# Sums of the gates' right operands formed behind two value blocks instead of in four attention units

## The chip, the core and the metric

One core of a Trainium2 chip runs the whole block. The time is the device time of one execution, in microseconds, and the figure that counts is the median of several. The engines are TensorE (PE, with its weight loads as PEld), VectorE (DVE), ScalarE (ACT), GpSimd (POOL) and SyncE (SP, which here only issues transfers). Each engine works through its own instructions in order; an instruction that waits holds all that stand behind it on its engine.

## The reference

One decoder block on x of 1024 rows (S) by 1024 channels (D), float32, with two attention branches of 512 channels each:

```
h    = rms_norm(x, g_pre)
proj = h @ w_in                          # q, k, v, z of both branches, forget logits, gates
ya   = fox_attention(qa, ka, va, log_sigmoid(fa + b_forget)) * silu(za)      # 8 heads of 64
yb   = diff_attention(rope(qb), rope(kb), vb, lam)                           # 4 heads, 2 x 64
yb   = rms_norm(yb, g_subln) * (1 - lam_init) * silu(zb)
gate_a, gate_b = split(sigmoid(gates))                                       # 1024 columns each
y    = (gate_a * (ya @ w_branch[0]) + gate_b * (yb @ w_branch[1])) @ w_out
out  = x + rms_norm(y, g_post)
```

All products are wanted to float32 accuracy. The kernel splits each operand into a high part (a cast) and a low part (the operand minus the cast), and adds three matmuls: high by high, high by low, low by high.

## The kernel before

**Value stage** (to about 112 us). `x_block(i)` normalizes 128 rows, transposes them and splits them into `hT`: eight tiles of 128 partitions by 4 by 512, indexed by part (high, low), half of the channels (kh) and half of the rows of x (sh). `v_block(i)` (L183 on) multiplies 128 rows with the value and forget columns, 72 matmuls into three accumulators `pv`, and brings the result out: ACT casts the high parts (L201, L207), DVE subtracts the low parts (L202, L208), SP stores `vbs` and `vas`. A loop over i calls `x_block(i + 3)` and `v_block(i)`, so all of `hT` is there once `v_block(4)` is reached. Blocks are counted from 0 in the code. The weights of this stage came through four slots of the pool `xp` named `wvraw`, which nothing uses after the weights are split.

**Attention** (to about 593 us). Eight units, 0 to 3 diff and 4 to 7 fox. `unit_proj(u)` multiplies the columns of q and k in two halves each (accumulators `pk`, `pq`, L246; two buffers `pj`; weights split by `load_w`, L234 and L236). For diff units `rope` copies the accumulator out and adds a rotated copy that SP moves between partitions; `stack` (L295 to L298) makes TA, TB, KA and KB. Each query row then has its score matmuls (`Sd` or `Sf`, L426) with a fused reduction on DVE (L428), an exponential on ACT (L433), scaling on POOL (L519, L549), transposes on PE (L455), and a product with the values (L479). The projections of the next unit, the products for z and, in fox units, other small tasks stand in a list `fill` that is worked off between the rows, to give PE something to do. Which instruction comes where on each engine is decided by a scheduler before the launch, from the order of the code, priorities and a simulated timeline; so a moved task moves its neighbours too.

**The combinations.** `h_combinations(k)` (L360 to L385), one for each k of 0 to 3, forms four sums or differences of the four quarters of h for one row tile of 128 channels: T5 = f12 - f11, T7 = f22 - f12, T6 = f22 - T5's tile, T4 = f21 - T6's tile, in the code's names, where each f is the sum of a high and a low quarter, made on POOL (L364). ACT casts the high part (L370), DVE makes the low part (L371), and SP stores each part by itself, 256 KB, in `t_d` in HBM (L373). The tiles are `raw` (three slots) and `sw` (two slots) of the pool `stg`, which the attention's own work shares. `TFILL` puts one call into the third place of `fill` in each of units 4 to 7.

**Gates.** `h_load` (L810) reads T4 to T7 back, 1 MB for each part, and the gate projections from the second on use them as right operands of a seven-product scheme in place of eight.

Of the kernel before, what the change touches and what calls it, by code (L numbers as in the profile page):

```python
# [9 lines left out]
F32 = mybir.dt.float32  # L10
F32R = mybir.dt.float32r
AF = mybir.ActivationFunctionType
ALU = mybir.AluOpType
# [3 lines left out]
P = 128  # L17
# [4 lines left out]
CH = 512  # L22
NEG = -1.0e30
SKEW = 1
SFILL = ((), (), (), (0,), (1,), (2,), (3,), ())
TFILL = ((), (), (), (), (0,), (1,), (2,), (3,))
UPR, DNR = slice(0, 64), slice(64, 128)
UP, DN = (0, 1, 2, 3), (3, 2, 1, 0)
GORD = (UP,) * 4 + (DN,) * 4
# [12 lines left out]
def f32(ap):  # L42
    return ap.bitcast(F32)
# [3 lines left out]
def tile_hybrid_block(  # L47
# [18 lines left out]
    nc = tc.nc  # L66
# [8 lines left out]
    dram = ctx.enter_context(tc.tile_pool(name="dram", bufs=1, space=DRAM))  # L75
# [21 lines left out]
    hT = [[[hpool.tile([P, 4, CH], F32R, tag=f"h{part}{kh}{sh}", name=f"hT{part}{kh}{sh}")  # L97
            for sh in range(2)] for kh in range(2)] for part in range(2)]
# [6 lines left out]
    ss_d = dram.tile([4, S], F32, name="ss_d")  # L105
    rs_d = dram.tile([4, S], F32, name="rs_d")
    z_d = [dram.tile([P, S], F32, name=f"z_d{t}") for t in range(8)]
    t_d = {m: [dram.tile([P, 4, CH], F32, name=f"t_d{m}_{part}") for part in range(2)]
           for m in (4, 5, 6, 7)}

    def rstd_of(dst, ss, n, eps):
        nc.gpsimd.tensor_scalar(dst, ss, 1.0 / n, eps, op0=ALU.mult, op1=ALU.add)
# [6 lines left out]
    with ExitStack() as st:  # L119
        vw = st.enter_context(tc.tile_pool(name="vw", bufs=1))  # L120
        xp = st.enter_context(tc.tile_pool(name="xp", bufs=2))
# [32 lines left out]
        def x_block(i):  # L154
            xs = wpool.tile([P, D], F32, tag="wraw", name=f"xs{i}")
            xg = xp.tile([P, D], F32, tag="xg", name=f"xg{i}", bufs=2)
            ss = small.tile([P, 1], F32, tag="ss", name=f"ss{i}")
            rs = small.tile([P, 1], F32, tag="rs", name=f"rs{i}")
            if i == 0:
                for half, acc in enumerate((rs, ss)):  # L160
                    hs = slice(half * CH, (half + 1) * CH)
                    nc.sync.dma_start(xs[:, hs], x2[0:P, hs])
                    nc.scalar.activation(xg[:, hs], xs[:, hs], AF.Square, accum_out=acc)
                nc.gpsimd.tensor_tensor(ss, ss, rs, op=ALU.add)
            else:
                nc.sync.dma_start(xs, x2[i * P:(i + 1) * P, :])
                nc.scalar.activation(xg, xs, AF.Square, accum_out=ss)
            rstd_of(rs, ss, D, EPS)
            for half in range(2):
                hs = slice(half * CH, (half + 1) * CH)  # L170
                nc.vector.scalar_tensor_tensor(
                    xg[:, hs], xs[:, hs], rs, g_bc[:, hs], op0=ALU.mult, op1=ALU.mult)
                tp = tps.tile([P, CH], F32, tag="tp", name=f"xt{i}_{half}")
                for q in range(4):
                    k = half * 4 + q
                    nc.tensor.transpose(tp[:, q * P:(q + 1) * P], xg[:, k * P:(k + 1) * P], ident)
                sl = slice(i % 4 * P, (i % 4 + 1) * P)
                tv = tp.rearrange("p (k s) -> p k s", k=4)
                hh, hl = (hT[part][half][i // 4][:, :, sl] for part in range(2))
                nc.scalar.copy(hh, tv)  # L180
                nc.vector.tensor_tensor(hl, tv, hh, op=ALU.subtract)  # L181

        def v_block(i):  # L183
# [26 lines left out]
            nc.vector.tensor_tensor(fg[:, i, :], ps[2][:, 256:264], bf_bc, op=ALU.add)  # L210
            nc.sync.dma_start(va_d[sl].rearrange("s a (b c) -> s (a b) c", b=2), f32(sa))

        x_block(0)
        for k in range(KT):
            load_wv(k)
# [3 lines left out]
        for i in range(NB):  # L219
            if i + 3 < NB:  # L220
                x_block(i + 3)
            v_block(i)


    def load_w(name, src, hi_act=False, lo_pool=False, pieces=None):
# [25 lines left out]
    with ExitStack() as st:  # L251
# [93 lines left out]
        def sum_squares(t, c):  # L345
# [10 lines left out]
            nc.tensor.matmul(ps, lhsT=onesr, rhs=lo, start=False, stop=True)  # L356
            nc.scalar.copy(sq[0:1], ps[0:1])
            nc.sync.dma_start(ss_d[t:t + 1, sl], sq[0:1])

        def h_combinations(k):  # L360

            def full(nm, kh, sh):
                t = stg.tile([P, CH], F32, tag="raw", name=f"f{nm}_{k}", bufs=3)
                nc.gpsimd.tensor_tensor(t, hT[0][kh][sh][:, k, :], hT[1][kh][sh][:, k, :], op=ALU.add)  # L364
                return t

            def parts(m, t):
                hi, lo = (stg.tile([P, CH], F32R, tag="sw", name=f"t{m}_{k}_{part}")
                          for part in range(2))
                nc.scalar.copy(hi, t)  # L370
                nc.vector.tensor_tensor(lo, t, hi, op=ALU.subtract)  # L371
                for part, p in enumerate((hi, lo)):
                    nc.sync.dma_start(t_d[m][part][:, k], f32(p))  # L373

            f11, f12 = full("11", 0, 0), full("12", 0, 1)
            nc.vector.tensor_tensor(f11, f12, f11, op=ALU.subtract)
            parts(5, f11)
            f22 = full("22", 1, 1)
            nc.vector.tensor_tensor(f12, f22, f12, op=ALU.subtract)
            parts(7, f12)  # L380
            nc.vector.tensor_tensor(f11, f22, f11, op=ALU.subtract)
            parts(6, f11)
            f21 = full("21", 1, 0)
            nc.vector.tensor_tensor(f21, f21, f11, op=ALU.subtract)
            parts(4, f21)  # L385

        def subln_scales(t):
            rs = sub_rs[:, t]
# [237 lines left out]
        for u in range(8):  # L626
            load, load_v, groups = nxt or unit_attn(u, T)
            nxt = None
            if u == 0:
                vload.append(load_v)  # L630
            if u == 1:
                forget_sums()
            load()
            fill = []
            if u + 1 < 8:
                T, tasks = unit_proj(u + 1)
                fill += tasks
            for t in ZFILL[u]:
                fill += z_tasks(t)
            fill[2:2] = [lambda k=k: h_combinations(k) for k in TFILL[u]]  # L640
            for t in SFILL[u]:
                fill += [lambda t=t, c=c: sum_squares(t, c) for c in range(2)]
                fill.append(lambda t=t: subln_scales(t))
            total = sum(s[0] for s in groups)
            done, nf = 0, 0
            for n, (wgt, rws, prd) in enumerate(groups):
                if n == len(groups) // 2 and u < 7:
                    nxt = unit_attn(u + 1, T)
                    vload.append(nxt[1])
                for r in rws:  # L650
                    r()
                if pend:
                    pend()
                pend = prd
                done += wgt
                while nf < len(fill) and nf < len(fill) * done / total:
                    fill[nf]()
                    nf += 1
# [145 lines left out]
    def h_load():  # L804

        ts = {m: [tpool.tile([P, 4, CH], F32R, tag=f"T{m}{part}", name=f"T{m}{part}")
                  for part in range(2)] for m in (6, 4, 7, 5)}
        for m in (4, 6, 5, 7):
            for part in range(2):
                nc.sync.dma_start(f32(ts[m][part]), t_d[m][part])  # L810
            h_ops[m] = [[t[:, k, :] for k in range(4)] for t in ts[m]]

    def gates_pair(d, order):
# [227 lines left out]
```

## Time and profile before

| | us |
|---|---|
| runs | 938.9, 936.02, 934.56 |
| median | 936.02 |
| span of the profiled execution | 932.1 |
| median less span | 3.9 |
| PE busy in the span | 890.1 |
| DVE, ACT, POOL busy | 625.5, 436.0, 486.6 |
| value stage ends (last `pv` matmul) | 111.7 |
| attention ends, gates begin | 593 |

The time of an execution holds the span, which is what the trace shows, and some microseconds around it that the trace does not show. In the rows of a timeline stand the start, the length, the engine, the line, the operation with what it writes and reads, and in brackets how long the engine had been idle before it and what ended that. A row of the waits names an engine and a line, what it waited for, and the total, the times and the longest. A row of groups has the busy total and the mean length in ns. A row of a table by stage has the stretch, its length, busy time and number of instructions on PE, PEld, DVE, ACT and POOL, the granted clock, the share of the DMA engines and GB/s.

### The profile page before, as it was taken

What the parts mean: (1) busy time and instruction counts of PE and PEld (TensorE: products, weight loads), DVE (VectorE), ACT (ScalarE), POOL (GpSimd) and SP (SyncE); (2) the same over time, 40 slices, a digit from 0 to 9 for tenths busy, and PEclk for the clock granted to TensorE, in tenths of its full rate; (3) what the DMA queues carried; (4) which work ended last, traced back from release to release, by engine and by line L of the source; (5) the groups of instructions that cost most, each with busy time, mean ns of one, the idle gap of its engine ahead of it and who ended that gap; (6) DMA issues with size and microseconds to landing.
All of it is one profiled execution on the core that took longest, in us unless ns stands there. A gap on an engine that the chain in (4) does not pass through costs nothing. (4 is left out here: it accounts for less than half of the span.)

```text
span 932.1 us, 13768 instructions
## 1 busy us (share of the span) xinstructions
PE 890.1 (95%) x4600; PEld 748.2 (80%) x4600; DVE 625.5 (67%) x1185; ACT 436.0 (47%) x861; POOL 486.6 (52%) x456
## 2 busy tenths in 40 slices
PE   7999999989999999999999998999999999999994
PEld 5899987777887878888878887788888878887873
DVE  6731257788878778577667568425668792559776
ACT  3421125556667574564755657523434450323331
POOL 7200034634745467373644566417677436878961
PEclk9999999999999999999999999999999999999997
DMA  8542346425334253544444342596655595211242
GB/s 314 185 139 93 114 124 160 115 69 138 98 92 142 71 179 104 157 128 124 147 153 129 98 161 72 221 396 193 197 167 174 184 362 198 71 44 46 91 135 90
DMA packets 118664, 136.95 MB, mean 147 GB/s; under 512 B 10545, under 2 KB 84273, under 8 KB 117570
## 3 DMA queue, kind: packets, MB, share of 16 engines
q1 hardware_dynamic: 118450, 135.82, 46.0%
q8 instruction: 36, 0.59, 0.3%
q14 instruction: 34, 0.28, 0.1%
q10 hardware_dynamic: 144, 0.26, 0.1%
HBM read 85.65 MB, written 37.81 MB: 132 GB/s over the span
## 5 line engine op out<-in xcount | busy, mean ns | idle before, releaser
L195 PE MATMUL pv<-wvhi,hT 128*128 128x264 f32 (+2 forms) x384 | 89.7, 326 | 0.4 <-DVE hT L181 0.4
L246 PE MATMUL pz<-hT,hi_z 128*128 128x512 f32 x256 | 83.9, 394 | 0.0
L246 PE MATMUL pk<-hT,hi_k 128*128 128x512 f32 x256 | 81.2, 394 | 2.0 <-DVE KB L298 2.0
L246 PE MATMUL pq<-hT,hi_q 128*128 128x512 f32 x256 | 82.3, 394 | 0.2 <-DVE TB L298 0.2
L727 PE MATMUL x_o<-wo_op,a_o 128*128 128x512 f32 x336 | 78.0, 392 | 3.4 <-POOL a_o L679 2.2
L861 PE MATMUL pb<-yT,hi_br 128*128 128x512 f32 x256 | 78.8, 390 | 0.1
L727 PEld LDWEIGHTS x_o<-wo_op,a_o 128*128 128x128 f32 x336 | 62.8, 188 | 18.5 <-POOL a_o L679 3.1
L727 PE MATMUL x_g<-T,a_g 128*128 128x512 f32 x336 | 77.5, 390 | 0.0
L727 PEld LDWEIGHTS x_g<-T,a_g 128*128 128x128 f32 x336 | 63.1, 188 | 13.3
L195 PEld LDWEIGHTS pv<-wvhi,hT 128*128 128x128 f32 x384 | 64.9, 191 | 6.3 <-DVE hT L181 0.7
L549 POOL TENSOR_SCALAR Pf<-Pf,lf 128x1024 f32<-128x1024 f32 (+3 forms) x64 | 50.2, 787 | 29.5 <-DVE lf L435 24.6
L433 ACT ACTIVATE Pd<-Pd,mxd 128x128 f32<-128x128 f32 (+7 forms) x64 | 49.6, 775 | 33.9 <-DVE mxd L428 33.2
L519 POOL TENSOR_SCALAR Pd<-Pd,ld 128x128 f32<-128x128 f32 (+7 forms) x32 | 26.1, 816 | 73.6 <-DVE ld L518 41.4
L545 POOL TENSOR_TENSOR cb<-cb,trim 128x128 f32<-128x128 f32 x64 | 31.1, 488 | 61.0 <-DVE mxf L428 39.8
L433 ACT ACTIVATE Pf<-Pf,mxf 128x1024 f32<-128x1024 f32 (+3 forms) x64 | 49.7, 777 | 27.3 <-DVE mxf L428 24.6
L195 PE MATMUL pv<-wvlo,hT 128*128 128x512 f32 (+2 forms) x192 | 62.0, 325 | 0.0
L727 PE MATMUL x_g<-hT,a_g 128*128 128x512 f32 x252 | 58.6, 390 | 0.0
L246 PEld LDWEIGHTS pk<-hT,hi_k 128*128 128x128 f32 x256 | 47.3, 188 | 12.0 <-DVE KB L298 2.4
L459 DVE TENSOR_TENSOR plf<-ptf,phf 128x512 fp32r<-128x512 f32 (+1 forms) x80 | 49.8, 633 | 10.2 <-ACT phf L458 9.7
L861 PEld LDWEIGHTS pb<-yT,hi_br 128*128 128x128 f32 x256 | 48.0, 188 | 10.5 <-DVE cu_g L720 0.6
L727 PEld LDWEIGHTS x_g<-hT,a_g 128*128 128x128 f32 x252 | 47.3, 188 | 10.0
L246 PEld LDWEIGHTS pq<-hT,hi_q 128*128 128x128 f32 x256 | 47.4, 188 | 9.4 <-PE pk L246 0.5
(247 smaller groups left out, 2419.4 us busy)
## 6 DMA issues: line engine op xcount, KB each, us to landing
t_d<-t SPq DMA_DIRECT2D x32, 256.0 KB, 2.1
T<-t_d SPq DMA_DIRECT2D x8, 1024.0 KB
raw<-in_w_in_dram SPq DMA_DIRECT2D x14, 512.0 KB, 4.2
vb_d<-vbs SPq DMA_DIRECT2D x8, 512.0 KB
va_d<-vas SPq DMA_DIRECT2D x8, 512.0 KB, 4.0
raw_k<-in_w_in_dram SPq DMA_DIRECT2D x8, 512.0 KB, 4.2
raw_q<-in_w_in_dram SPq DMA_DIRECT2D x8, 512.0 KB
V<-vb_d SPq DMA_DIRECT2D x4, 1024.0 KB
```

The source lines that it names most:

```text
L195: nc.tensor.matmul(ps[n], lhsT=hT[hp][k // 4][i // 4][:, k % 4, hs], rhs=wt[k][:, a:b], start=first, stop=(k == KT - 1 and hp == 1))
L246: nc.tensor.matmul(ps, lhsT=a[:, k, :], rhs=hT[h][k // 4][c][:, k % 4, :], start=(k == 0 and a is hi and h == 0), stop=(k == KT - 1 and a ...
L433: nc.scalar.activation(pr[:, 0:n], pr[:, 0:n], AF.Exp, bias=mx[:, len(pcs) - 1:len(pcs)], scale=-1.0, accum_out=le)
L459: nc.vector.tensor_tensor(pl[:, 0:n], pt[:, 0:n], ph[:, 0:n], op=ALU.subtract)
L519: nc.gpsimd.tensor_scalar(p2[:, 0:n], p2[:, 0:n], l2, 1.0, op0=ALU.mult, op1=ALU.mult)
L545: nc.gpsimd.tensor_tensor(diag, diag, trim, op=ALU.add)
L549: nc.gpsimd.tensor_scalar(p1[:, 0:n], p1[:, 0:n], l1, 1.0, op0=ALU.mult, op1=ALU.mult)
L727: nc.tensor.matmul(x[m], lhsT=a[:, ai, k, :], rhs=right[m][bi][k], start=(k == 0 and n == 0), stop=(k == 3 and n == 2))
L861: nc.tensor.matmul(ps, lhsT=a[:, kk, :], rhs=yT[g][h][:, k % 2, sl], start=(k == 0 and a is hi and h == 0), stop=(k == 3 and a is lo))
```

## The change

`h_combinations` moves into the value stage. `TBLK` calls it for k = 0 and 1 behind `v_block(4)` and for k = 2 and 3 behind `v_block(5)` (value blocks 5 and 6, counted from 1). The arithmetic is the same: per row tile 4 adds on POOL, 4 subtractions and 4 low parts on DVE, 4 casts on ACT. The tiles come from the four `wvraw` slots: `fa` and `fb` hold two f each, and each T has one tile with both parts. One transfer of 512 KB stores an operand's tile, 16 in place of 32, and it is issued from ACT's queue and not from SP's. In HBM both parts of an operand stand in one array, and `h_load` reads the same bytes.

```diff
-TFILL = ((), (), (), (), (0,), (1,), (2,), (3,))
+TBLK = ((), (), (), (), (0, 1), (2, 3), (), ())
...
-    t_d = {m: [dram.tile([P, 4, CH], F32, name=f"t_d{m}_{part}") for part in range(2)]
-           for m in (4, 5, 6, 7)}
+    t_d = {m: dram.tile([P, 2, 4, CH], F32, name=f"t_d{m}") for m in (4, 5, 6, 7)}
...
+        def h_combinations(k):
+
+            fa = xp.tile([P, 2, CH], F32, tag="wvraw", name=f"fa_{k}", bufs=4)
+            fb = xp.tile([P, 2, CH], F32, tag="wvraw", name=f"fb_{k}", bufs=4)
+            f11, f12, f22, f21 = fa[:, 0], fa[:, 1], fb[:, 0], fb[:, 1]
+
+            def full(t, kh, sh):
+                nc.gpsimd.tensor_tensor(t, hT[0][kh][sh][:, k, :], hT[1][kh][sh][:, k, :], op=ALU.add)
+
+            def parts(m, t):
+                p = xp.tile([P, 2, CH], F32R, tag="wvraw", name=f"t{m}_{k}", bufs=4)
+                nc.scalar.copy(p[:, 0], t)
+                nc.vector.tensor_tensor(p[:, 1], t, p[:, 0], op=ALU.subtract)
+                nc.scalar.dma_start(t_d[m][:, :, k], f32(p))
+
+            full(f11, 0, 0)
+            full(f12, 0, 1)
+            nc.vector.tensor_tensor(f11, f12, f11, op=ALU.subtract)
+            parts(5, f11)
...
             v_block(i)
+            for k in TBLK[i]:
+                h_combinations(k)
...
-        def h_combinations(k):
...
-                hi, lo = (stg.tile([P, CH], F32R, tag="sw", name=f"t{m}_{k}_{part}")
-                          for part in range(2))
-                nc.scalar.copy(hi, t)
-                nc.vector.tensor_tensor(lo, t, hi, op=ALU.subtract)
-                for part, p in enumerate((hi, lo)):
-                    nc.sync.dma_start(t_d[m][part][:, k], f32(p))
...
-            fill[2:2] = [lambda k=k: h_combinations(k) for k in TFILL[u]]
...
-                nc.sync.dma_start(f32(ts[m][part]), t_d[m][part])
+                nc.sync.dma_start(f32(ts[m][part]), t_d[m][:, part])
```

The lines behind the diff's first part have other numbers in the changed kernel (L201 becomes L200, L236 becomes L265, L298 becomes L327). The scheduler's order moves at three places that the prediction speaks of. First ACT's order from the fifth value block on (`vbs4`, `vas4`: the evacuations of block 4). Before:

```order
L201 CAST vbs4_854<-pv4_0_779 128x4x128
L207 CAST vas4_858<-pv4_1_780 128x4x64
L207 CAST vas4_858<-pv4_2_781 128x4x64
L201 CAST vbs5_940<-pv5_0_865 128x4x128
L207 CAST vas5_944<-pv5_1_866 128x4x64
```

and the same place in the changed kernel, where a DMA row is the issue of a store:

```order
L223 CAST t5_0_866<-fa_0_861 128x512
L225 DMA t_d5_134<-t5_0_866 256x1x512
L223 CAST t7_0_872<-fa_0_861 128x512
L200 CAST vbs4_850<-pv4_0_775 128x4x128
L225 DMA t_d7_136<-t7_0_872 256x1x512
L223 CAST t6_0_877<-fa_0_861 128x512
L206 CAST vas4_854<-pv4_1_776 128x4x64
L225 DMA t_d6_135<-t6_0_877 256x1x512
L223 CAST t4_0_883<-fb_0_862 128x512
L206 CAST vas4_854<-pv4_2_777 128x4x64
L225 DMA t_d4_133<-t4_0_883 256x1x512
```

Four casts and four issues of row tile 0 now stand between and around the three evacuations of block 4; row tiles 1 to 3 stand in the same way at blocks 5, 6 and 7. An issue waits for the low part from DVE, and the third cast of a tile waits for the first store to land, since it takes that store's slot. Second, DVE's order at the end of the value stage, before:

```order
L202 TENSOR_TENSOR vbs7_1112<-pv7_0_1037,vbs7_1112 128x4x128
L236 TENSOR_TENSOR lo_k0_1180<-raw_k0_1177,hi_k0_1179 128x1024
L208 TENSOR_TENSOR vas7_1116<-pv7_1_1038,vas7_1116 128x4x64
L208 TENSOR_TENSOR vas7_1116<-pv7_2_1039,vas7_1116 128x4x64
L210 TENSOR_TENSOR fg_84<-pv7_2_1039,bf_bc_81 128x8
L236 TENSOR_TENSOR lo_q0_1225<-raw_q0_1222,hi_q0_1224 128x1024
```

and in the changed kernel (`t7_3`, `t6_3`, `t4_3`: low parts of row tile 3; `lo_k0`, `lo_q0`: the low weights of unit 0's projections):

```order
L224 TENSOR_TENSOR t7_3_1036<-fa_3_1025,t7_3_1036 128x512
L201 TENSOR_TENSOR vbs7_1212<-pv7_0_1137,vbs7_1212 128x4x128
L224 TENSOR_TENSOR t6_3_1041<-fa_3_1025,t6_3_1041 128x512
L265 TENSOR_TENSOR lo_k0_1280<-raw_k0_1277,hi_k0_1279 128x1024
L207 TENSOR_TENSOR vas7_1216<-pv7_1_1138,vas7_1216 128x4x64
L224 TENSOR_TENSOR t4_3_1047<-fb_3_1026,t4_3_1047 128x512
L207 TENSOR_TENSOR vas7_1216<-pv7_2_1139,vas7_1216 128x4x64
L209 TENSOR_TENSOR fg_84<-pv7_2_1139,bf_bc_81 128x8
L265 TENSOR_TENSOR lo_q0_1325<-raw_q0_1322,hi_q0_1324 128x1024
```

The low weights of unit 0 now stand behind the low parts of the last row tile, and POOL's high weights `hi_k0` and `hi_q0` behind all 16 adds. Third, DVE's order in unit 6, where unit 7's projection is brought out (`t4_2`: the low part of T4 for row tile 2), before:

```order
L371 TENSOR_TENSOR t4_2_1_5543<-f21_2_5539,t4_2_0_5542 128x512
L296 TENSOR_TENSOR TA7_5388<-pq7_0_5483,TA7_5388 64x512
L298 TENSOR_TENSOR KB7_5391<-pk7_0_5448,KB7_5391 64x512
L559 TENSOR_TENSOR ys5_2_5102<-ypf5_1_2_5173,yt5_1_2_5212 64x256
L428 ISA Pf5_1_0_5357,mxf5_1_0_5358<-Sf5_1_0_0_5359,cb5_1_4598 128x128
```

and in the changed kernel:

```order
L461 TENSOR_TENSOR plf5_0_1_0_5284<-ptf5_0_1_0_5282,phf5_0_1_0_5283 128x512
L327 TENSOR_TENSOR KB7_5419<-pk7_0_5476,KB7_5419 64x512
L430 ISA Pf5_1_1_5374,mxf5_1_1_5375<-Sf5_1_1_0_5376,cb5_1_4662 128x256
L430 ISA mxf5_1_1_5375 128x1
L561 TENSOR_TENSOR ys5_2_5158<-ypf5_1_2_5201,yt5_1_2_5240 64x256
L461 TENSOR_TENSOR plf5_0_1_1_5293<-ptf5_0_1_1_5291,phf5_0_1_1_5292 128x384
L325 TENSOR_TENSOR TA7_5416<-pq7_0_5511,TA7_5416 64x512
```

No operation of the combinations stands ahead of KB7 any more, and TA7 has gone behind it. The order of PE moves too: before, unit 0's projections stand as 24 matmuls of each of `pk`, `pq`, `pk`, `pq` and 10 of the next unit's `pk` ahead of the first score; in the changed kernel 24 `pk`, 2 `pq`, 22 `pk`, 22 `pq`, 2 `pk`, 24 `pq`, and then 24 and 10 of the next unit's ahead of the first score. From the gates on, the order of every engine is the same in both.

More of the change, by code (lines that the diff above doesn't have):

```diff
@@ L211, in v_block @@
             nc.sync.dma_start(va_d[sl].rearrange("s a (b c) -> s (a b) c", b=2), f32(sa))
+        def h_combinations(k):
[13 more added lines that the diff above has]
+            parts(5, f11)
+            full(f22, 1, 1)
+            nc.vector.tensor_tensor(f12, f22, f12, op=ALU.subtract)
+            parts(7, f12)
+            nc.vector.tensor_tensor(f11, f22, f11, op=ALU.subtract)
+            parts(6, f11)
+            full(f21, 1, 0)
+            nc.vector.tensor_tensor(f21, f21, f11, op=ALU.subtract)
+            parts(4, f21)
         x_block(0)
@@ L358, in sum_squares @@
             nc.sync.dma_start(ss_d[t:t + 1, sl], sq[0:1])
-        def h_combinations(k):
[L362 to L367, printed above, removed]
-                hi, lo = (stg.tile([P, CH], F32R, tag="sw", name=f"t{m}_{k}_{part}")
-                          for part in range(2))
-                nc.scalar.copy(hi, t)
-                nc.vector.tensor_tensor(lo, t, hi, op=ALU.subtract)
-                for part, p in enumerate((hi, lo)):
[L373 to L385, printed above, removed]
         def subln_scales(t):
```

## The prediction

> **What bounds the kernel now.** I read the page's head first, then the busy table by stage, then the waits of TensorE (PE), and last the timelines at the two ends of the stretch that the change touches.
>
> ```profile
> span 932.1 us, 13768 instructions
> PE 890.1 (95%) x4600; PEld 748.2 (80%) x4600; DVE 625.5 (67%) x1185; ACT 436.0 (47%) x861; POOL 486.6 (52%) x456
> ```
>
> PE is busy for 890.1 of 932.1 us. The change adds and removes no matmul, so it can gain only from the 42 us in which PE is idle, from a lower clock, or lose by making PE wait where it does not now. The next table says where that idle time lies (stretch; its length; busy time and count of PE, weight loads, DVE, ACT, POOL; granted clock; DMA share; GB/s).
>
> ```profile
> 80.00:100.00 20.00, 20.00 (x134) 18.34 (x133) 2.73 (x6) 2.29 (x5) 1.04 (x1) 1.00 0.23 94
> ...
> 134.00:215.00 81.00, 75.28 (x379) 61.01 (x378) 65.32 (x145) 46.04 (x96) 39.84 (x34) 1.00 0.46 119
> 215.00:556.00 341.00, 334.74 (x1868) 286.17 (x1867) 250.45 (x611) 207.16 (x432) 188.16 (x199) 1.00 0.44 130
> 556.00:593.00 37.00, 31.78 (x211) 26.90 (x210) 30.87 (x94) 29.55 (x67) 21.85 (x32) 0.95 0.20 63
> ```
>
> While the last value blocks are multiplied (80 to 100 us here) PE has no gap, and DVE, ACT and POOL are nearly free. In the attention, PE is idle 5.7 us in 134 to 215 (units 0 and 1), 6.3 in 215 to 556 and 5.2 in 556 to 593. The combinations run in units 4 to 7, so at most the last two figures are theirs to give back. The waits of PE say that many short waits make them up (total, times, longest):
>
> ```profile
> PE Sd L426 <- DVE mxd L428: 5.0, 10, 0.8
> PE Sf L426 <- DVE mxf L428: 2.0, 3, 0.9
> PE pk L246 <- DVE KB L298: 2.0, 1, 2.0
> ```
>
> The `Sd` waits belong to the diff units 0 to 3, where no combination runs. `Sf` and the single wait of `pk` lie in fox units, and both are for DVE.
>
> **The change part by part.** What moves, by groups (busy us, mean ns):
>
> ```profile
> L364 POOL TENSOR_TENSOR f<-hT,hT 128x512 f32<-128x512 f32 x16 | 22.8, 1426 | 5.7 <-DMA z_d<-sz 3.6 <-DMA ss_d<-sq 2.0
> L370 ACT CAST t<-f 128x512 fp32r<-128x512 f32 x16 | 9.9, 619 | 21.5 <-issue 5.4 <-DMA t_d<-t 5.2 <-DVE lf L435 3.6
> L371 DVE TENSOR_TENSOR t<-f,t 128x512 fp32r<-128x512 f32 x16 | 14.6, 915 | 6.8 <-DMA t_d<-t 3.4 <-ACT t L370 2.6 <-ACT Pf L433 0.5
> L379 DVE TENSOR_TENSOR f<-f,f 128x512 f32<-128x512 f32 x4 | 5.7, 1428 | 0.5 <-POOL f L364 0.5
> ```
>
> Out of units 4 to 7 go 16 adds on POOL (22.8 us), 16 casts on ACT (9.9), 16 low halves on DVE (14.6) and 16 subtractions there: by their mean of 0.9 to 1.4 another 15. Most of these 30 us of DVE cost PE nothing today, since filler matmuls cover them. They cost where a low half waits in DVE's queue for the store that holds its slot (`DMA t_d<-t 3.4`) and something urgent stands behind it. This happens once with filler about:
>
> ```profile
> 479.17 0.69 DVE L371 TENSOR_TENSOR t<-f,t 128x512 fp32r<-128x512 f32 x1 [0.92 <-DMA t_d<-t]
> 479.89 0.69 DVE L296 TENSOR_TENSOR TA<-pq,TA 64x512 fp32r<-64x512 f32 x1
> 480.61 0.69 DVE L298 TENSOR_TENSOR KB<-pk,KB 64x512 fp32r<-64x512 f32 x1
> 481.36 0.73 PE L246 MATMUL pk<-hT,hi_k 128*128 128x512 f32 x2 [1.99 <-DVE KB L298]
> ```
>
> DVE idles 0.92 us for the store and spends 0.69 on the low half; KB, which frees the accumulator that the next `pk` needs, is 1.61 late from these two alone, and an earlier wait of the same kind precedes it. In the new order no combination stands ahead of KB. Term 1: **-1.9 us** of the 1.99.
>
> The second place is unit 7, after the last filler:
>
> ```profile
> 551.33 0.86 DVE L384 TENSOR_TENSOR f<-f,f 128x512 f32<-128x512 f32 x1 [1.09 <-DMA t_d<-t]
> 554.09 0.69 DVE L371 TENSOR_TENSOR t<-f,t 128x512 fp32r<-128x512 f32 x1 [1.29 <-DMA t_d<-t]
> 557.55 0.67 DVE L371 TENSOR_TENSOR t<-f,t 128x512 fp32r<-128x512 f32 x1
> 558.81 0.50 PE L426 MATMUL Sf<-KB,TB 128*128 128x512 f32 x1 [0.88 <-DVE mxf L428]
> 560.89 0.50 PE L426 MATMUL Sf<-KA,TA 128*128 128x512 f32 x1 [0.86 <-DVE mxf L428]
> 563.01 1.41 PE L455 MATMUL ptf<-ident,Pf 128*128 128x128 f32 x6 [0.43 <-POOL Pf L549]
> ```
>
> DVE stands 2.38 us for stores here and works 2.2 us on the last three rows of row tile 3, just ahead of the reductions that PE then waits for: 0.88 + 0.86 + 0.43 = 2.17 us. When this goes, the softmax of the last rows (exponential on ACT, scale on POOL, transpose, low half) is late next, and it has no filler either way. I take two thirds. Term 2: **-1.4 us**. Behind these waits the clock dips:
>
> ```profile
> 562.00:564.00 2.00, 1.52 (x9) 1.29 (x8) 1.94 (x8) 0.54 (x3) 2.00 (x3) 0.80 0.52 125
> 564.00:566.00 2.00, 2.00 (x10) 2.00 (x10) 1.81 (x6) 1.70 (x3) 1.31 (x3) 0.50 0.83 235
> 566.00:568.00 2.00, 2.00 (x16) 1.86 (x15) 1.68 (x7) 1.92 (x6) 1.14 (x2) 0.85 0.00 0
> ```
>
> At 0.80, 0.50 and 0.85 the 6 us lose 0.4 + 1.0 + 0.3 = 1.7 us. The Trainium skill (TensorE: Matmul & The Clock Gate, on the two states) says that the clock halves after an idle window of about 3.4 us; here the trace shows it after gaps that together last less, the longest 0.88, so by the rule no dip would be due and by the trace one is. Whether shorter gaps avoid it is a coin toss: term 3, **-0.8**. The other waits of units 4 to 6 are scattered and small; I give them **-0.3**.
>
> The order of the whole attention also shifts: the first scores come 24 projection matmuls later, and more filler is used in unit 0 (267 filler matmuls before the 48th row of scores instead of 246; equal from unit 2 on: 624 and 624 before the 192nd). Units 0 and 1 hold 5.7 us of idle time, which this can shrink or stretch: -1 to +3. Term 4: **+0.7**.
>
> Now what is added. Behind blocks 4 to 7 each row tile has 4 adds on POOL, 8 operations on DVE, 4 casts and 4 stores on ACT, in a chain through four slots: low half, store, landing, next use of the slot. Each of ACT's waits stands ahead of the evacuations of a value block, and the last tile ahead of unit 0's weights. The rows there today:
>
> ```profile
> 66.63 1.29 DVE L181 TENSOR_TENSOR hT<-xt,hT 128x512 fp32r<-128x512 f32 x2 [0.15 <-ACT hT L180]
> ...
> 94.66 0.59 ACT L201 CAST vbs<-pv 128x512 fp32r<-128x512 f32 x1 [5.19 <-PE pv L195]
> ...
> 105.97 0.58 ACT L201 CAST vbs<-pv 128x512 fp32r<-128x512 f32 x1 [5.17 <-PE pv L195]
> 107.20 1.22 DVE L236 TENSOR_TENSOR lo_k<-raw_k,hi_k 128x1024 fp32r<-128x1024 f32 x1
> 111.54 0.63 PE L246 MATMUL pk<-hT,hi_k 128*128 128x512 f32 x2
> 112.01 0.40 PE L246 MATMUL pk<-hT,lo_k 128*128 128x512 f32 x1
> ```
>
> And the costs of one store, one issue on ACT and one add, from the groups' details (ns: least, median, most) and the page's list of DMA issues:
>
> ```profile
> L373 SPq DMA_DIRECT2D t_d<-t x32: 319/320/576, 350.4 to 558.3; - x32
> DMA to landing us min/median/max: 2.1/2.1/4.4
> ```
>
> ```profile
> va_d<-vas SPq DMA_DIRECT2D x8, 512.0 KB, 4.0
> L976 ACTq DMA_DIRECT2D out_dram<-go x1: 378/378/378, 928.9 to 928.9; - x1
> L364 POOL TENSOR_TENSOR f<-hT,hT x16: 1302/1310/2307, 337.1 to 549.5; 128x512 f32<-128x512 f32 x16
> ```
>
> `lo_k` is done at 108.42 and first read at 112.01: 3.6 us of room. In the new order it stands behind the third low half of the last tile. No row shows a 512 KB store of such a tile, so its landing is bounded by 2.1 us (the median of the 256 KB stores of the same data) and 4.0 (the 512 KB `va_d` stores); I take 4.0, the same size. An issue on ACT takes 0.38. By hand I laid the four tiles through the three queues from 67.9 us on, when the last x block is split (66.63 + 1.29), with 0.69 for a DVE operation (the rows at 479 to 481), the median of 1.31 for an add, 0.62 for a cast, and the evacuations at their 11.3 us rhythm (94.66 to 105.97). With a landing of 2.1 or 3.0 the chain fits: `lo_k` is ready by 110, in time. With 4.0 it is ready at 113.5 to 114, and PE waits 1.5 to 2.0 us at its first `lo_k`. With 4.0 and longer durations (0.85 and 1.43, near the means of 0.915 and 1.426, which hold the cases where DVE and POOL held each other up) it is ready at 117.7, a wait of 5.7. `lo_q`, last of all, is covered, since the new order has two matmuls of `pq` and then 22 of the second `pk` (about 5 us) ahead of its first use. Term 5: **+1.8 us**, ends 0 and +5.7. The Trainium skill (DMA: Bandwidth & Descriptors, on the anatomy of one DMA) speaks against the change: a semaphore wait is held by the issuing sequencer, before dispatch. By it, every store that waits for its low half holds ACT's evacuations behind it; the hand count already does so. The same section's estimate for a transfer, 2.0 us and bytes by 436 GB/s, would give 3.2 us for 512 KB, and with that term 5 would be near 0.
>
> SP loses 32 issues and stays idle mostly; 16 of 512 KB move the same 8 MB, so the loads at 592 us are unchanged. Both are worth nothing. From 600 us on the order is the same.
>
> Sum against the profiled 932.1: -1.9 - 1.4 - 0.8 - 0.3 + 0.7 + 1.8 = -1.9, so 930.2. The median of the runs shown, 936.02, is 3.9 above the span; with this added the forecast is **934.1 us**. About 0.5%, 4.7 us, is what a measurement of this kernel can tell from no change, so faster means under 931.3 and slower over 940.7.
>
> **The rivals.**
> (a) *All of the cover is found.* Landings near 3 us keep the value stage free of waits (term 5 zero), unit 7's 2.17 us and the dip of 1.7 go whole, 1.5 us of the small fox waits go with the 1.9, and the new order costs nothing: -7.3, or 928.7. For it: 30 us of DVE leave a stretch in which DVE is the releaser named most. Against: those waits have the softmax chain next behind DVE.
> (b) *Nothing is won.* PE is covered in the fox units by filler, and the waits at 481 and 558 come back a little later with another releaser, while unit 0 loses a microsecond: 936 to 937. For it: each gain is a single event of 2 us. Against: the row at 481 names KB behind a stalled low half plainly.
> (c) *Slower: ACT's queue makes the last tile late.* Landings of 4.0 us and colliding DVE and POOL operations stack over the four tiles, `lo_k` is ready at 117.7 or, with the slowest landing of today's stores (4.4), at 119.3; PE stands 5.7 to 7.3 us at 112, long enough for a dip of 1.7 like the one above. With terms 1 to 4 kept (-3.7) this gives +3.7 to +5.3: 939.7 to 941.3, say 941. It decides from a `lo_k` that ends later than about 117. For it: ACT holds each store behind a wait with the evacuations behind it. Against: each tile has a block of 11.3 us, and DVE is busy in it for 2.7 of 20 now.
> (d) *The change does not do what it says*: the order shows that it does, so no chance is kept for it.
>
> **How the numbers follow.** The forecast gets 0.42, (a) 0.22, (b) 0.17, (c) 0.19. The range reaches from (a), 928.5, to the upper figure of (c), 941.5; what is beyond is about 2 in 10. Faster by over 0.5% is (a) and a little of the forecast's lower side: 0.27. Slower by over 0.5% is most of (c): 0.16. The rest, 0.57, is within.
>
> **What would show it.** Right: no `t_d` wait on DVE after 130 us, no 2 us wait of `pk` near 481, `Sf` waits at 558 smaller, and a wait of `pk` for `lo_k` near 112 of 0 to 2 us. Term 5 is wrong if that wait is over 4 us, or if PE waits inside the value stage for a `pv` buffer; the store rows of ACT then land in over 4 us. Terms 1 and 2 are wrong if PE's idle time from 215 to 593, 11.5 us now, does not fall by 3. Term 4 is wrong if units 0 and 1 idle more than 8 or less than 4.

## The result and the profile after

The changed kernel takes 941.05 us in the median of four runs (939.27 to 942.45), against 935.29 in four runs before (a fourth, of 934.38, beside the three shown above): slower by a factor of 1.0056, 95% interval 1.0034 to 1.0078. Measured once more beside other kernels it was 940.56 (ratio 1.0067, 1.0041 to 1.0093). The forecast was 934.1, and the upper end of the range, 941.5, held it, but the direction was the other one. It came out as rival (c) had it, in its sign and its size, though only in part for its reasons. All medians and ratios here are of fast executions, without three that took over 3 ms.

The head of the page of the changed kernel:

```profile
span 937.5 us, 13738 instructions
PE 892.3 (95%) x4600; PEld 747.2 (80%) x4600; DVE 621.0 (66%) x1185; ACT 435.5 (46%) x861; POOL 480.7 (51%) x456
```

The span is 5.4 us longer. To see where, I cut both traces at the first `pk` matmul, at 134, at 350 and at the first gate matmul (`pg`). The two times in between are not quite the same place in both: the first fox score stands at 340.9 before and at 353.2 after, 12 us later. Cut at that score, the idle time of the fox units comes out the same within 0.2 us. Stretch, length, busy time of PE, PEld, DVE, ACT and POOL, clock, DMA. Before:

```profile
111.54:134.00 22.46, 22.46 (x101) 18.59 (x100) 9.89 (x13) 5.01 (x9) 5.86 (x4) 1.00 0.32 88
134.00:350.00 216.00, 207.65 (x1100) 173.15 (x1099) 171.89 (x423) 136.72 (x281) 115.52 (x98) 1.00 0.45 122
350.00:592.97 242.97, 234.12 (x1356) 200.90 (x1355) 174.72 (x425) 146.04 (x313) 134.30 (x167) 0.99 0.40 123
```

After:

```profile
111.10:134.00 22.90, 18.42 (x74) 14.35 (x72) 10.50 (x21) 4.12 (x10) 2.79 (x2) 0.93 0.58 178
134.00:350.00 216.00, 205.36 (x1064) 168.36 (x1062) 163.72 (x395) 127.75 (x264) 109.22 (x91) 0.99 0.43 117
350.00:599.66 249.66, 243.99 (x1419) 209.61 (x1419) 157.00 (x427) 147.57 (x318) 116.01 (x160) 1.00 0.32 92
```

The stretch from `pk` to `pg` takes 481.43 us before and 488.56 after, 7.1 more (from `pg` to the end the second trace is 1.3 shorter; the order there is the same in both, and over all runs of this study that stretch lies between 337.2 and 339.1). PE's idle time goes from 0 to 4.5 us in the first part, from 8.4 to 10.6 in the second, from 8.9 to 5.7 in the third. The clock, summed over windows of 2 us as (1 - clock) times busy time, costs 1.7 in the first, 1.7 in the second and none in the third, where it cost 1.6 before. So the beginning lost 4.5 + 1.7, the diff units 2.3 + 1.7, and the fox units gained 3.2 + 1.6. That is +5.4 of the 7.1; the other 1.7 lies in longer matmuls, and I could not place it.

The waits of PE after the change (total, times, longest) show the same:

```profile
PE pk L275 <- DVE lo_k L265: 4.3, 1, 4.3
...
PE ypd L481 <- DVE pld L461: 3.6, 2, 2.7
PE Sd L428 <- DVE mxd L430: 3.0, 8, 0.6
...
PE Sf L428 <- DVE mxf L430: 0.9, 2, 0.6
```

The 2.0 us wait of `pk` for KB is gone and `Sf` is down from 2.0 to 0.9. In their place stand a wait of 4.3 for the low weights of unit 0 and one of 2.7 for a low half in unit 1. The first, on PE, and DVE's work ahead of it, with POOL's row beside the third of the long ones:

```profile
116.03 0.63 PE L275 MATMUL pk<-hT,lo_k 128*128 128x512 f32 x1 [4.26 <-DVE lo_k L265]
```

```profile
105.36 0.69 DVE L229 TENSOR_TENSOR fa<-fa 128x512 f32<-128x512 f32 x1 [0.94 <-POOL fa L219]
106.74 1.64 DVE L224 TENSOR_TENSOR t<-fa,t 128x512 fp32r<-128x512 f32 x1 [0.69 <-ACT t L223]
108.30 1.78 DVE L232 TENSOR_TENSOR fa<-fb,fa 128x512 f32<-128x512 f32 x1
110.00 1.52 DVE L234 TENSOR_TENSOR fa<-fb,fa 128x512 f32<-128x512 f32 x1
...
114.76 1.22 DVE L265 TENSOR_TENSOR lo_k<-raw_k,hi_k 128x1024 fp32r<-128x1024 f32 x1
```

```profile
109.50 1.49 POOL L263 TENSOR_SCALAR hi_k<-raw_k 128x1024 fp32r<-128x1024 f32 x1
```

The rows of DVE down to 110.00 are operations of row tile 3. Three of them take 1.5 to 1.8 us in place of 0.69. The first two run while POOL makes its last two adds (106.54 to 109.53), the third beside POOL's `hi_k`. `lo_k` comes out at 115.98; before, it was done at 108.42. The clock behind the gap:

```profile
116.00:118.00 2.00, 1.97 (x5) 1.57 (x6) 1.00 (x3) 0.43 (x2) 0.39 (x1) 0.56 0.99 345
118.00:120.00 2.00, 2.00 (x6) 1.54 (x6) 0.41 (x2) 0.00 (x0) 0.65 (x1) 0.58 0.81 167
```

Why the last tile comes so late is read from POOL's adds, one pair of `fa` for each of tiles 1, 2 and 3 (tile 0 starts at 66.95):

```profile
77.63 2.98 POOL L219 TENSOR_TENSOR fa<-hT,hT 128x512 f32<-128x512 f32 x2 [6.43 <-DMA t_d<-t]
...
89.93 2.99 POOL L219 TENSOR_TENSOR fa<-hT,hT 128x512 f32<-128x512 f32 x2 [6.37 <-DMA t_d<-t]
...
102.30 3.03 POOL L219 TENSOR_TENSOR fa<-hT,hT 128x512 f32<-128x512 f32 x2 [5.80 <-DMA t_d<-t]
```

Tile 1 starts 10.7 us behind tile 0 and the others 12.3 and 12.4 us behind the one ahead, where a value block takes 11.3. Each of them waits for a store of the tile ahead (`t_d<-t`), whose slot it takes. The stores themselves are as forecast; they land in 3.1, 3.8 and 4.6 us (least, median, most):

```profile
L225 ACTq DMA_DIRECT2D t_d<-t x16: 520/521/580, 71.8 to 116.9; - x16
...
DMA to landing us min/median/max: 3.1/3.8/4.6
```

The wait in unit 1, on DVE and on PE:

```profile
205.01 4.05 DVE L605 TENSOR_TENSOR fs<-fs 128x64 f32<-128x64 f32 x1
...
209.72 0.55 DVE L461 TENSOR_TENSOR pld<-ptd,phd 128x384 fp32r<-128x384 f32 x1
```

```profile
210.32 0.39 PE L481 MATMUL ypd<-pld,V 128*128 128x256 f32 x1 [2.75 <-DVE pld L461]
```

POOL beside it:

```profile
205.37 1.28 POOL L318 TENSOR_TENSOR swk<-swk,sinT 128x512 f32<-128x512 f32 x1
206.62 2.35 POOL L524 TENSOR_TENSOR Pd<-Pd,Pd 128x1024 f32<-128x1024 f32 x1
```

and, in the kernel before, the same product, and the wait of PE for the same sums:

```profile
196.78 0.21 DVE L603 TENSOR_TENSOR fs<-fs 128x64 f32<-128x64 f32 x1
```

```profile
PE ft L615 <- DVE fs L606: 1.8, 1, 1.8
```

A product of 128 by 64 in the forget sums takes 4.05 us and ends with POOL's two operations; the low half that PE needs stands behind it. In the order before, the same product takes 0.21 us, and another one, of the same helper, 1.03. There PE waits 1.8 us for the transposes of these sums (`ft`), a wait that is gone in the changed kernel. So the sums cost 0.9 us of idle time more than before, and the dip.

### The profile page after: what moved, and what is told of

The parts are those of the page before. It is cut to its first block, busy times and chain, and to the rows that moved or that the text cites. A ratio compares the mean times of both kernels' runs of the same rounds, so it can differ in the third digit from the quotient of the medians.

```text
span 937.5 us, 13738 instructions
## 1 busy us (share of the span) xinstructions
PE 892.3 (95%) x4600; PEld 747.2 (80%) x4600; DVE 621.0 (66%) x1185; ACT 435.5 (46%) x861; POOL 480.7 (51%) x456
## 5 line engine op out<-in xcount | busy, mean ns | idle before, releaser
L275 PE MATMUL pk<-hT,hi_k 128*128 128x512 f32 x256 | 84.3, 405 | 1.6 <-ACT sq L386 0.6
L728 PEld LDWEIGHTS x_g<-T,a_g 128*128 128x128 f32 x336 | 63.1, 188 | 13.3
L521 POOL TENSOR_SCALAR Pd<-Pd,ld 128x128 f32<-128x128 f32 (+7 forms) x32 | 28.0, 876 | 71.7 <-DVE ld L520 42.3
L551 POOL TENSOR_SCALAR Pf<-Pf,lf 128x1024 f32<-128x1024 f32 (+3 forms) x64 | 47.6, 748 | 28.3 <-DVE lf L437 25.9
L460 ACT CAST phf<-ptf 128x512 fp32r<-128x512 f32 (+1 forms) x80 | 42.5, 542 | 40.9 <-PE ptf L457 33.5
L430 DVE CUSTOM_DVE_ANT_0 Pf<-Sf,cb 128x512 f32<-128x512 f32 (+1 forms) x64 | 36.4, 570 | 34.3 <-PE ptf L457 24.0
```

The lines of the kernel that those rows point to most:

```text
L275: nc.tensor.matmul(ps, lhsT=a[:, k, :], rhs=hT[h][k // 4][c][:, k % 4, :], start=(k == 0 and a is hi and h == 0), stop=(k == KT - 1 and a ...
L430: nc.vector.tensor_tensor_reduce(out=pr[:, a:b], in0=ps, in1=bias[:, boff + a:boff + b], scale=-0.125, scalar=BIG if j == 0 else mx[:, j - ...
L460: nc.scalar.copy(ph[:, 0:n], pt[:, 0:n])
L521: nc.gpsimd.tensor_scalar(p2[:, 0:n], p2[:, 0:n], l2, 1.0, op0=ALU.mult, op1=ALU.mult)
L551: nc.gpsimd.tensor_scalar(p1[:, 0:n], p1[:, 0:n], l1, 1.0, op0=ALU.mult, op1=ALU.mult)
L728: nc.tensor.matmul(x[m], lhsT=a[:, ai, k, :], rhs=right[m][bi][k], start=(k == 0 and n == 0), stop=(k == 3 and n == 2))
```

## The experiments

Theories: **S**, a tile's chain through four slots is longer than a value block. **L**, it is so because DVE and POOL hold each other up in these operations. **Q**, ACT's queue holds evacuations behind stores. **M**, found on the way: the attention's first tiles lie over the slots. **H**, the wait at 210 is a collision by itself. **P** and **V** are stated with their run. Ratios are against the kernel before, timed on the same chip.

**Six slots**

```diff
-name=f"fa_{k}", bufs=4     (and fb, t, wvraw)
+name=f"fa_{k}", bufs=6
```

> The wvraw tag gets six slots and not four; nothing else in the source changes. Theory S (slots): in the changed kernel a tile's chain takes 12.3 us (adds start at 77.6, 89.9, 102.3) against 11.3 for a value block, because the next tile's adds wait for the store of t7 to land; with six slots that link is cut, so the wait of pk for lo_k (4.3 us) and the low clock behind it (1.7) go: about 935, and about 931 if the wait of ypd at 210 (2.75 and its dip of 1.7) moves away too. Rival Q (the queue of ACT holds evacuations and casts behind stores): the wait stays at 3 us or more, 939 to 941. Rival L (DVE and POOL hold each other up in these operations): the wait stays as well, since all operations are the same.

Measured: 934.03 (0.9979, 0.9962 to 0.9996). The later tiles start 10.1 to 10.2 us apart and the last low half ends at 108.8, as S said. But PE still waits 4.2 us for `lo_k`, with another releaser ahead of it on DVE:

```profile
116.80 0.23 DVE L584 TENSOR_TENSOR lt<-lt 128x64 f32<-128x64 f32 x1 [5.71 <-DMA lt<-in_lambda_k_dram]
116.95 1.22 DVE L265 TENSOR_TENSOR lo_k<-raw_k,hi_k 128x1024 fp32r<-128x1024 f32 x1
```

```profile
SPq L581 <- DMA t_d<-t: 3.2, 1, 3.2
```

DVE stands for the loads of the lambda vectors. Their tile `lt` belongs to the attention's pool `pp`, and SP issues the loads between 112.7 and 115.5, after it has stood 3.2 us for the last store of a combination. In the kernel before, DVE had used them by 72.6. That is theory M: the stage's slots, in use longer, hold up what is laid over them. Two links had to be cut and I had cut one. The 7 us by which the median is better than the changed kernel's come from elsewhere. Part of it can be seen: PE's order in units 0 and 1 is the old one again, without the wait at 210 and its dip. The rest cannot, since the profiled execution was the slowest of the twelve.

**Stores from SP**

```diff
-                nc.scalar.dma_start(t_d[m][:, :, k], f32(p))
+                nc.sync.dma_start(t_d[m][:, :, k], f32(p))
```

> The changed kernel with the sixteen stores issued from SP's queue. Q: the wait of pk for lo_k goes, 935. S: landings and slots are as before, the chain loses the issue time on ACT alone (0.5 us of each link at most), so the wait is 2.5 to 4.3 us and the time 939 to 941. L: no difference, 941.

Measured: 938.11 (1.0030, 1.0015 to 1.0044), between what Q and S gave and nearer to S. The wait stays, 1.1 us shorter:

```profile
PE pk L275 <- DVE lo_k L265: 3.1, 1, 3.1
```

ACT's queue, which the change names and rival (c) blamed, is 1.1 us of the 4.26. Behind it come new waits of 1.0 for `lo_q` and 0.7 for `rawq`, but no low clock there in this trace. Q falls as the main cause.

**Adds on DVE**

```diff
-                nc.gpsimd.tensor_tensor(t, hT[0][kh][sh][:, k, :], hT[1][kh][sh][:, k, :], op=ALU.add)
+                nc.vector.tensor_tensor(t, hT[0][kh][sh][:, k, :], hT[1][kh][sh][:, k, :], op=ALU.add)
```

> The changed kernel with the sixteen adds of the combinations on DVE and none on POOL. L: the subtractions and low halves fall from 1.0 to 1.8 us to 0.69, a tile's chain from 12.3 to about 9.3 us, shorter than a value block, and the wait of pk for lo_k goes: 935. S without L (the landing of 3.8 us alone makes the chain too long): the wait stays over 2.5 us, 938 or more. Q: no difference, 941.

Measured: 936.69 (1.0018, 1.0005 to 1.0031). With four slots, ACT's stores and nearly the same order of PE, but no adds on POOL beside DVE, `lo_k` is in time and its wait is gone:

```profile
109.56 1.22 DVE L265 TENSOR_TENSOR lo_k<-raw_k,hi_k 128x1024 fp32r<-128x1024 f32 x1
...
120.25 1.23 DVE L265 TENSOR_TENSOR lo_q<-raw_q,hi_q 128x1024 fp32r<-128x1024 f32 x1 [6.27 <-DMA va_d<-vas]
```

S holds only with the adds on POOL: DVE alone gets through all of the work sooner than DVE and POOL together. From the first add of the last tile to the end of `lo_k` it takes 10.6 us here and 13.7 in the changed kernel. The groups of the low halves, in the changed kernel and here:

```profile
L224 DVE TENSOR_TENSOR t<-fa,t 128x512 fp32r<-128x512 f32 x12 | 10.2, 850 | 5.5 <-ACT t L223 5.5
```

```profile
L224 DVE TENSOR_TENSOR t<-fa,t 128x512 fp32r<-128x512 f32 x12 | 8.2, 686 | 2.3 <-ACT t L223 2.2
```

This run changes two things at once: the collisions go, and an add takes about 0.65 us on DVE where it took 1.3 to 1.8 on POOL. No run parts the two. What is left of the loss is not `lo_q`: DVE stands 6.27 us ahead of it for the store of the last `vas`, whose buffer it takes, but PE does not wait for it. It is a new wait of 2.85 us of `pq` at 132, and the wait at 210 (2.74), which is there too:

```profile
131.87 0.72 PE L275 MATMUL pq<-hT,hi_q 128*128 128x512 f32 x2 [2.85 <-ACT rawq L312]
```

```profile
SPq L581 <- DMA t_d<-t: 6.3, 1, 6.3
```

SP stands 6.3 us, until 120.61, ahead of the loads of lambda, and issues the moves of unit 0's rope only behind them; ACT copies `rawq`, for which PE waits, behind that rope's last casts. This fits theory M, on another path; no run here has both the adds on DVE and the early loads. So 936.7 and not 935.

**Two tiles in the value stage, two in units 4 and 5**

```diff
-TBLK = ((), (), (), (), (0, 1), (2, 3), (), ())
+TBLK = ((), (), (), (), (0,), (1,), (), ())
+TFILL = ((), (), (), (), (2,), (3,), (), ())
```

> Row tiles 0 and 1 behind value blocks 4 and 5, row tiles 2 and 3 in the fill of units 4 and 5 as in the kernel before. S: two chains of 12.3 us end by 93, so no wait for lo_k; the wait near 481 and those of unit 7 are gone as in the changed kernel, units 4 and 5 give back at most 1.5 us: 932 to 934, 3 to 4 more if the wait near 210 stays. A rival that blames the new order of the attention and not the end of the value stage: 938 or more, with idle time between 134 and 350 above 10 us.

Measured: 928.23 (0.9922, 0.9904 to 0.9940), better than either kernel and 3.8 us below the range that I gave. PE has no gap at 112 and no dip, and the fox units keep the whole gain, though two tiles still run in units 4 and 5; I had expected these to cost something:

```profile
111.04:134.00 22.96, 22.96 (x104) 18.98 (x103) 10.45 (x13) 5.20 (x9) 6.38 (x5) 1.00 0.32 88
134.00:350.00 216.00, 207.39 (x1102) 173.24 (x1100) 172.70 (x423) 136.95 (x281) 115.74 (x97) 1.00 0.44 122
350.00:586.29 236.29, 231.40 (x1353) 198.94 (x1352) 163.13 (x409) 140.64 (x304) 119.95 (x159) 1.00 0.36 109
```

**Three tiles, one in unit 4**

```diff
+TBLK = ((), (), (), (), (0, 1), (2,), (), ())
+TFILL = ((), (), (), (), (3,), (), (), ())
```

> Row tiles 0 and 1 behind value block 4, row tile 2 behind block 5, row tile 3 in the fill of unit 4. S: three chains of 12.3 us end by about 104, ahead of lo_k, so PE waits under 1 us at 112 and the time is that of two tiles, 928 to 930. Theory M (memory: the loads of the lambda vectors, whose tile lies over the slots, wait for the last stores, and DVE waits for these loads ahead of lo_k): the wait is 2 us or more and the time 931 to 934.

Measured: 934.77 (0.9989, 0.9971 to 1.0007), just above M's range, and with M's wait. The third chain ends at 103.3, in time, yet PE waits 3.9 us for `lo_k` and loses 1.7 to the clock:

```profile
111.36 0.23 DVE L612 TENSOR_TENSOR lt<-lt 128x64 f32<-128x64 f32 x1 [6.59 <-DMA lt<-in_lambda_k_dram]
...
114.70 1.23 DVE L266 TENSOR_TENSOR lo_k<-raw_k,hi_k 128x1024 fp32r<-128x1024 f32 x1
```

**Three tiles, lambda early**

```diff
-        lt = pp.tile([P, 4, 64], F32, tag="P", name="lt")       (in the attention)
+        lt = xp.tile([P, 4, 64], F32, tag="xg", name="lt", bufs=2)   (ahead of the loop over the blocks)
```

> Three row tiles in the value stage as before, with the lambda vectors loaded and summed early in the stage. M: the 3.9 us wait for lo_k and its low clock of 1.7 were the loads of lambda, so both go: 934.8 less 5.6, about 929. S: the third chain itself holds lo_k: the wait stays over 2 us, 932 or more.

Measured: 926.72 (0.9913, 0.9881 to 0.9946): the wait and the clock are gone, 7 to 8 us less than without the edit (each against the kernel before on its own chip). That is some 2 us more than the wait and the dip come to; their source is open.

```profile
105.37 0.69 DVE L202 TENSOR_TENSOR vbs<-pv,vbs 128x512 fp32r<-128x512 f32 x1 [1.70 <-ACT vbs L201]
108.19 1.23 DVE L278 TENSOR_TENSOR lo_k<-raw_k,hi_k 128x1024 fp32r<-128x1024 f32 x1 [2.13 <-DMA va_d<-vas]
```

**Six slots, lambda early**: both edits on all four tiles.

> Six slots, and the lambda vectors loaded and summed behind the weights' loads in the value stage, in a slot of xg, so that nothing of it stands between the last combinations and lo_k. S with M: with both links cut no wait of pk at 112 and no low clock, 934.0 less 4.2 and 2.3, about 928. If another link makes lo_k late (L, Q): the wait stays over 2 us and the time over 932.

Measured: 931.09 (0.9969, 0.9950 to 0.9988). Better than six slots alone by about 3 us and not by 6.5: of the wait 1.2 us is left, and 1.9 for `lo_q`, and a dip of 1.7 follows. The link now is the store of `vas`, whose buffer the low weights take:

```profile
111.39 1.23 DVE L277 TENSOR_TENSOR lo_k<-raw_k,hi_k 128x1024 fp32r<-128x1024 f32 x1 [3.15 <-DMA va_d<-vas]
...
119.02 1.23 DVE L277 TENSOR_TENSOR lo_q<-raw_q,hi_q 128x1024 fp32r<-128x1024 f32 x1 [5.67 <-DMA va_d<-vas]
```

The `vas` of block 6 is stored from 106.61, since its evacuation stands behind the last tile's work on ACT and DVE. That may be a share of Q's mechanism after all; no run takes it apart.

**Four slots, lambda early**: the changed kernel with this edit alone.

> The changed kernel (four tiles, four slots) with the lambda vectors loaded and summed early, as in the kernels of three tiles and of six slots. S: in the changed kernel the loads of lambda come behind lo_k and cost nothing there, so the wait of about 4.3 us for lo_k and its low clock stay; the rope of unit 0, ahead of which DVE stood for lambda, starts earlier and gives back 1 us at most: 938 to 941. M: the wait for lo_k falls below 2 us, 934 or less.

Measured: 941.89 (1.0068, 1.0043 to 1.0092), no better than the changed kernel, wait and all:

```profile
117.17 0.49 PE L287 MATMUL pk<-hT,lo_k 128*128 128x512 f32 x1 [4.26 <-DVE lo_k L277]
```

So in the changed kernel it is the chain, and M waits behind it. Slow landings are not the reason either: the stores land in 3.1 to 3.5 us here, and PE waits as long. Of the four corners (four or six slots, lambda late or early: 941, 934, 942 and 931) the early loads pay only where the slots are not the longer link.

**Lambda early in the kernel before**: the control.

> The kernel before with the lambda vectors loaded and summed early and nothing else: a control. No wait of it stands on a critical engine before, so 934 to 937, no change; if it gains more than 3 us by itself, that much of the gain of three tiles with early lambda is not the tiles'.

Measured: 934.50 (0.9991, 0.9974 to 1.0009). No change, so the early loads gain nothing by themselves; they pay only together with the tiles.

**Two tiles, stores from SP**

> Two row tiles in the value stage as in the kernel of two tiles, their eight stores issued from SP. Q: where nothing is late, ACT's queue costs nothing; 928, no change.

Measured: 929.31 (0.9943, 0.9922 to 0.9964); the interval overlaps that of the stores from ACT. Where nothing is late, the issuing queue makes no difference that these runs can tell.

**No tile in the value stage, two each in units 4 and 5**

```diff
-TFILL = ((), (), (), (), (0,), (1,), (2,), (3,))
+TFILL = ((), (), (), (), (0, 1), (2, 3), (), ())
```

> The kernel before with its four combinations still in the attention, two each in units 4 and 5 and none in 6 and 7. Theory P (what pays is that units 6 and 7, whose filler runs out, are free of them): the waits at 481 and 558 to 563 go and units 4 and 5, covered by filler, give back 2 us at most: 929 to 932. Rival V (what pays is that DVE has two tiles less in the attention at all): units 4 and 5 wait for stores as unit 6 did, 933 to 936.

Measured: 937.55 (1.0022, 1.0001 to 1.0044), worse than I gave either theory. The profiled execution was the slowest of the twelve. The waits that P names are gone in it (none over 0.9 us from 460 to the gates, and no dip). But the combinations now wait for their stores in units 4 and 5,

```profile
391.71 0.69 DVE L371 TENSOR_TENSOR t<-f,t 128x512 fp32r<-128x512 f32 x1 [1.73 <-DMA t_d<-t]
433.71 1.01 DVE L371 TENSOR_TENSOR t<-f,t 128x512 fp32r<-128x512 f32 x1 [1.50 <-DMA t_d<-t]
```

and PE's idle time from 350 to the gates rises from 8.9 to 11.1 us all the same. It also rises from 134 to 350 (8.4 to 11.1), where no combination runs in either kernel; that part I can't explain. P's forecast falls: units 6 and 7 free of combinations do not pay when these come on top of those of units 4 and 5. What free units would pay by themselves this run doesn't show.

**Forget sums in unit 2**, in the changed kernel and in that of two tiles.

```diff
-            if u == 1:
+            if u == 2:
                 forget_sums()
```

> The changed kernel with the forget sums called in unit 2 and not in unit 1. Theory H (the wait of ypd at 210 is a forget product on DVE that stands behind POOL's last add of unit 1): that wait of 2.75 us and its dip of 1.7 go, some 1.8 come back as a wait of the forget transposes in unit 2: 937 to 939, the wait for lo_k at 112 unchanged. Rival (the new order of the attention as a whole is worse): idle time and low clock between 134 and 350 stay near 12 us, 941.

Measured: 936.38 (1.0009, 0.9990 to 1.0029), near H's figure. But the trace, of the slowest of the ten runs, doesn't carry H: the wait of 2.75 at 210 is gone, and new ones of 1.67 at 222, 1.72 at 304 (with a dip of 1.6) and 1.23 at 311 stand in its place, with the same span, 937.5. The wait for `lo_k` is unchanged at 4.25.

> Two row tiles in the value stage and two in units 4 and 5, with the forget sums in unit 2. H: the 2.6 us wait of the forget transposes in unit 1 moves to unit 2, where it may find cover: 926 to 928. Rival (the wait is the same wherever it stands): 928.

Measured: 935.88 (1.0011, 0.9992 to 1.0031), about 8 us worse than with the sums in unit 1. Idle time from 134 to 350 is 13.3 us where it was 8.6, and the clock costs 3.1 where it cost nothing. Both theories missed. A task of a dozen small DVE operations moves as much time through the order of the diff units as the whole change does.

**The changed kernel again**

> The changed kernel itself once more, beside the next three on one chip, since its time rests on four runs and the profiles of single runs differ by 2 to 3 us: 939 to 942, with the wait for lo_k near 4 us and the wait of ypd at 210 as in the first profile.

Measured: 940.56, with 4.27 at `lo_k` and 2.75 at 212. Against the trace of the kernel before, this second one loses 4.5 us of idle time and 2.8 of clock at the beginning and 0.6 and 2.9 from 134 to 350, and gains 2.9 and 1.6 behind. The three parts of the account come back in it; in the diff units nearly all of the loss is in the clock.

## Why the prediction was wrong

Terms 1 to 3 and the scatter (-4.4) were right. The fox units gained 3.2 us of idle time and 1.6 of clock, -4.8. Of the wait of `pk` behind KB 0.4 is left, and the three waits at 558 to 563 and the dip are gone. I had kept back a third of those three waits and half of the dip, and all of both went.

**Term 5 failed in its size, and with it the sign of the sum.** I took +1.8 and the traces show 4.26 of wait and 1.7 of clock, +6.0. The landing of 4.0 was right (3.8 measured), the issue on ACT nearly (0.52 for 0.38). The aside with 3.2 us for a landing used an estimate that the Trainium skill (DMA: Bandwidth & Descriptors, on the anatomy of one DMA) gives for transfers issued by GpSimd; ACT's stores took 3.1 to 4.6. What failed is "with 0.69 for a DVE operation ... the median of 1.31 for an add" as the likely case. These figures come from the fox units, where the adds and subtractions of one tile are scattered among other work. Put next to each other they meet in every tile: the first subtraction of tiles 0 and 1 and the second of tile 2 take 1.76 to 1.77, and in the last tile three operations in a row take 1.5 to 1.8. I had this as the outer end ("longer durations"); it was the case.

The first three tiles take 35.4 us from start to start, 1.5 more than three value blocks, and the last takes 13.7 from its start to the end of `lo_k` at 115.98. Of these, 2.9 are what its three long operations take over 0.69. Six slots bring the starts 10.1 to 10.2 us apart with the collisions kept, and with the lambda loads out of the way too the wait falls to 1.2, so the four slots are needed for the loss. Adds on DVE take the wait away with the slots kept, so POOL's adds are needed too, by their collisions or by their own length. Stores from SP take 1.1 us. So it is slots together with POOL's adds, and ACT's queue, by which (c) is named, is the smaller part.

Rival (c) had the sign, the time, the place and the collisions right. That its figure of 941 was met is in part luck: it gave 5.7 to 7.3 of wait and 1.7 of clock, where 4.26 and 1.7 came, and kept term 4 at +0.7, where +4.0 came. Its point of decision, `lo_k` later than 117, was a microsecond too late.

**Term 4 failed too.** I took +0.7 with ends of -1 and +3; from 134 to 350 it was +2.3 of idle time and +1.7 of clock. The other waits from 134 to 215 hardly changed (3.8 us before, 3.3 after). The forget sums in unit 1 are most of the loss: a wait of 2.75 us with its dip in place of one of 1.83 without. The wait of 2.75 stands in each of the kernels with this order of PE and the forget sums in unit 1 (changed, stores from SP, adds on DVE, early lambda alone) and in none with the old order. That it comes with the new order is shown; that a better place of the forget sums cures it isn't, since these moved other waits. My two tests for terms 1, 2 and 4 were badly cut. Idle time from 215 to the gates mixes diff and fox units: it fell by 1.3 only, for the diff units took back part of what the fox units gave. And 134 to 215 went from 5.7 to 6.1 only, though the 2.75 lies in it, since the older wait of 1.83 is gone and the dip is no idle time.

**What I had not seen** is the link through memory. Slots in use up to 117 hold up whatever the next stage lays over them; in the changed kernel it hides behind the chain, in three tiles and in six slots it is the one that ends last.

The three-tile kernel with early lambda (926.7) and the two-tile kernel (928.2) beat both the kernel before and the changed one, and their intervals overlap. Moving two tiles, or three with the lambda vectors out of the way, was worth 7 to 8 us; four were one or two too many.

## What to carry to other kernels

An idle engine is a place for work only up to the next hand-over: count the chain through its buffers per step against the step that it should hide in, and stop moving work when the last step would reach the next stage's first operands. Price operations of engines that hold each other up by their durations side by side, not by the median of scattered ones. When scratch slots live longer, list what the next stage lays over them, since the first load there waits for the last store.

## What the runs showed of the hardware

DVE operations with two operands in SBUF and POOL operations on such tiles stretch each other: a subtraction of 128x512 goes from 0.69 to 1.76 us next to POOL's adds, one of these adds from 1.28 to 1.77, and a product of 128x64 from 0.21 to 4.05 when two POOL operations (1.28 and 2.35 us) run meanwhile. The Trainium skill (SBUF — State Buffer, on the two separate sides) says that a DVE operation with two SBUF inputs and a GpSimd operation that reads SBUF take the shared ports as an exclusive lock for the whole instruction. The subtractions agree with it, as do the 0.69 us of the low halves once POOL has no adds. The product agrees in part: it starts 0.36 us ahead of the first of the two POOL operations and yet ends behind both, in all five traces that have it. Why, no run shows.

The clock of PE fell to about 0.57 for 4 us behind a gap of 4.26 us, and to 0.50 and 0.69 for 4 us behind one of 2.75. The latter is shorter than the window of about 3.4 us that the Trainium skill (TensorE: Matmul & The Clock Gate, on the two states) gives. Not every gap is followed by one: not the 3.1 us at `lo_k` with stores from SP, nor the 2.75 in unit 1 of the kernel with four slots and early lambda. Of the 13 gaps of 2.7 to 4.3 us in the attention of these traces, 11 cost 1.5 to 2.9 us more than themselves, and a prediction should carry that. Shorter gaps can have a dip too: one of 1.44 us had it in the kernel of two tiles with the forget sums in unit 2, and gaps of 1.43 to 1.45 at the same place had none in three other kernels.
